# RMSNorm with SiLU: 48 KB blocks in four buffers, no look-ahead, and rstd moved from VectorE to the Silu

## Chip, cores, metric

One core of one Trainium2 chip. The time is the device time of one execution in microseconds (us). The profile's span (from the first to the last instruction) is 1.7 to 1.8 us shorter than the time of the same run. An execution of a one-core kernel is called slow when it is over 1.5% above the fastest of its kernel; all comparisons below use fast runs, except where it is said.

## The reference

```python
# x: (8, 1024, 2048) float32, gamma: (2048,), eps: 1e-5
rms = np.sqrt(np.mean(x ** 2, axis=-1, keepdims=True) + eps)
out = gamma * x / rms
return (out * (1 / (1 + np.exp(-out)))).astype(np.float32)
```

8192 rows of 2048 floats: 67.1 MB in, 67.1 MB out, and only a few operations per element.

## The kernel before

The rows are cut into 16 blocks of 512. Each of the 128 partitions holds four consecutive rows of a block, one run of 32 KB, and there are six such buffers. A load goes out on the queue of SyncE, a store on that of ScalarE. The order of work looks one block ahead: the square sums of block b+1 come before the multiplies of block b.

```python
J = 4
BUFS, LEAD = 6, 6
...
def sums(b, after_first=()):
    ...                                     # half of the rows on VectorE: sum of squares into ss
    for j in range(na):                     # the other half on ScalarE
        nc.scalar.activation(out=junk_a, in_=row(b, j), func=ACT.Square, accum_out=ss[:, j:j + 1])
        if j == 0:
            for s in after_first:
                store(s)                    # store of b-1 behind the first square of b+1
    nc.scalar.activation(out=rms, in_=ss, func=ACT.Sqrt, scale=1.0 / d, bias=eps_t)
...
def finish(b, halves=False):
    for j in range(J):
        nc.vector.scalar_tensor_tensor(out=row(b, j), in0=row(b, j), scalar=rstds[b][:, j:j + 1],
                                       in1=g, op0=ALU.mult, op1=ALU.mult)
        if j % 2:                           # Silu over two rows at once
            nc.scalar.activation(out=blocks[b][:, cols], in_=blocks[b][:, cols], func=ACT.Silu)
            ...                             # the last block is stored in two halves
def store(b):
    nc.scalar.dma_start(out=ob[b], in_=blocks[b])
    if b + LEAD < nblk:
        load(b + LEAD)
...
for b in range(1, last - 1):
    sums(b + 1, after_first=[b - 1])
    finish(b)
    invert(b + 1)                           # rstd = 1 / rms
```

Of the kernel before, what the change touches and what calls it, by code (L numbers as in the profile page):

```python
# [1 line left out]

# [4 lines left out]

ACT = mybir.ActivationFunctionType
ALU = mybir.AluOpType


@with_exitstack
def kernel(
    ctx: ExitStack,
    tc: tile.TileContext,
    x: bass.AP,
    gamma: bass.AP,
    eps: bass.AP,
    out: bass.AP,
):  # L20





    nc = tc.nc
    P = nc.NUM_PARTITIONS
    f32 = mybir.dt.float32
    x2 = x.flatten_outer_dims()
    o2 = out.flatten_outer_dims()  # L30
    n, d = x2.shape
    J = 4
    BUFS, LEAD = 6, 6
    nblk = n // (P * J)
    xb = x2.rearrange("(b p j) d -> b p (j d)", p=P, j=J)
    ob = o2.rearrange("(b p j) d -> b p (j d)", p=P, j=J)

    singles = ctx.enter_context(tc.tile_pool(name="singles", bufs=1))
    pool = ctx.enter_context(tc.tile_pool(name="pool", bufs=BUFS))
    small = ctx.enter_context(tc.tile_pool(name="small", bufs=2))  # L40
    psum = ctx.enter_context(tc.tile_pool(name="psum", bufs=1, space=bass.MemoryType.PSUM))

    g = singles.tile([P, d], f32)
    eps_t = singles.tile([P, 1], f32)
    ones = singles.tile([P, P], f32)
    junk_a = psum.tile([P, d], f32, name="junk_a")
    junk_v = psum.tile([P, d], f32, name="junk_v")
    blocks, rmss, rstds = {}, {}, {}

    def load(b):  # L50
        xt = pool.tile([P, J * d], f32, name="xt")
        nc.sync.dma_start(out=xt, in_=xb[b])  # L52
        blocks[b] = xt

    def row(b, j):
        return blocks[b][:, j * d:(j + 1) * d]

    def sums(b, after_first=()):


        ss = small.tile([P, J], f32, name="ss")
        na = J // 2
        for j in range(na, J):
            nc.vector.tensor_tensor_reduce(  # L64
                out=junk_v, in0=row(b, j), in1=row(b, j), scale=1.0, scalar=0.0,
                op0=ALU.mult, op1=ALU.add, accum_out=ss[:, j:j + 1])
        for j in range(na):
            nc.scalar.activation(out=junk_a, in_=row(b, j), func=ACT.Square,  # L68
                                 accum_out=ss[:, j:j + 1])
            if j == 0:  # L70
                for s in after_first:
                    store(s)
        rms = small.tile([P, J], f32, name="rms")
        nc.scalar.activation(out=rms, in_=ss, func=ACT.Sqrt, scale=1.0 / d, bias=eps_t)  # L74
        rmss[b] = rms

    def invert(b):
        rstd = small.tile([P, J], f32, name="rstd")
        nc.vector.reciprocal(out=rstd, in_=rmss.pop(b))  # L79
        rstds[b] = rstd  # L80

    def finish(b, halves=False):
        for j in range(J):
            nc.vector.scalar_tensor_tensor(out=row(b, j), in0=row(b, j), scalar=rstds[b][:, j:j + 1],  # L84
                                           in1=g, op0=ALU.mult, op1=ALU.mult)
            if j % 2:
                cols = slice((j - 1) * d, (j + 1) * d)
                nc.scalar.activation(out=blocks[b][:, cols], in_=blocks[b][:, cols], func=ACT.Silu)  # L88
                if halves:
                    nc.scalar.dma_start(out=ob[b][:, cols], in_=blocks[b][:, cols])  # L90

    def store(b):
        nc.scalar.dma_start(out=ob[b], in_=blocks[b])  # L93
        if b + LEAD < nblk:
            load(b + LEAD)

    with tc.manual_schedule():


        Q = 4  # L100
        w = d // Q
        grow = pool.tile([P, J * d], f32, name="xt")
        for b in range(BUFS - 1):
            load(b)
        nc.vector.memset(ones, 1.0)  # L105
        nc.vector.memset(eps_t, float(eps))  # L106
        nc.scalar.activation(out=junk_a[:, 0:1], in_=ones[:, 0:1], func=ACT.Square)  # L107
        nc.scalar.dma_start(out=grow[0:P:P // Q, 0:w],
                            in_=bass.AP(tensor=gamma.tensor, offset=gamma.offset, ap=[[w, Q], [1, w]]))
        for c in range(Q):  # L110
            k = c * (P // Q)
            nc.tensor.matmul(junk_v[:, c * w:(c + 1) * w], ones[k:k + 1, :], grow[k:k + 1, 0:w],  # L112
                             start=True, stop=True)
        nc.vector.tensor_copy(out=g, in_=junk_v)  # L114
        load(BUFS - 1)


        last = nblk - 1
        sums(0)
        invert(0)  # L120
        finish(0)
        sums(1)
        invert(1)
        for b in range(1, last - 1):
            sums(b + 1, after_first=[b - 1])
            finish(b)
            invert(b + 1)
        store(last - 2)
        finish(last - 1)
        store(last - 1)  # L130
        sums(last)
        invert(last)
        finish(last, halves=True)


# [1 line left out]
_INS = ['x', 'gamma', 'eps']  # L137
_OUTS = [((8, 1024, 2048), 'float32')]

_NUMBERS = {'eps': 9.999999747378752e-06}  # L140


# [26 lines left out]
```

## Time and profile before

| what | before |
|---|---|
| time, median | 317.8 us (317.19 to 318.23, 6 runs) |
| span of the profiled run | 316.3 us |
| share of the span that the DMA packets take | 49.7% + 49.2% |
| VectorE, ScalarE busy | 71%, 71% |
| median time from issue to landing of a load, of a store | 42.0 us, 35.2 us |

A transfer is called landed here at the last semaphore event that the trace has for it (in the kernel before 0.34 us after the end of the last packet of the first load). Read the two DMA shares first: they add to 98.9%, and nothing else is near that.

### The profile page before, as it was taken

How to read it: one execution, taken by the hardware profiler on the slowest of the kernel's cores; microseconds unless marked ns; L12 is line 12 of the kernel's file. 1: busy time of each engine (PE TensorE's matmuls, PEld its weight loads, DVE VectorE, ACT ScalarE, POOL GpSimd, SP SyncE). 2: the span in 40 equal slices, each digit the busy share in tenths (PEclk: the TensorE clock that was granted, in tenths of full speed). 3: DMA queues.
4: the chain of work that ended last, by engine and by line, in shares of the span. 5: the costliest groups of instructions: out<-in, count | busy, mean ns of one | idle time of the engine just before them, and what ended most of it. 6: DMA issues, size and time to landing. Idle time of an engine off the chain costs nothing.

```text
span 316.3 us, 444 instructions
## 1 busy us (share of the span) xinstructions
PE 2.1 (1%) x8; PEld 0.5 (0%) x8; DVE 223.5 (71%) x147; ACT 223.8 (71%) x144; POOL 0.2 (0%) x4
## 2 busy tenths in 40 slices
PE   0200000000000000000000000000000000000000
PEld 0000000000000000000000000000000000000000
DVE  0679499999493983939849397593966939993900
ACT  1357958999967777678676687676786776879540
POOL 0000000000000000000000000000000000000000
DMA  8999999999999999999999999999999999999996
GB/s 328 402 464 410 452 390 410 452 419 443 439 424 452 411 452 410 452 414 456 406 456 414 448 414 448 439 423 452 414 452 410 452 414 456 406 456 410 452 407 269
DMA packets 4763, 134.25 MB, mean 425 GB/s; under 512 B 532, under 2 KB 532, under 8 KB 536
## 3 DMA queue, kind: packets, MB, share of 16 engines
q1 hardware_dynamic: 2304, 67.11, 49.7%
q10 hardware_dynamic: 2456, 67.12, 49.2%
q14 instruction: 3, 0.02, 0.0%
HBM read 67.12 MB, written 67.11 MB: 424 GB/s over the span
## 4 chain that ended last, share of the span: by engine, by line
DMA 74%; DVE 14%; ACT 5%; issue 2%; DVEq 1%; ACTq 0%; SPq 0%
DMA xt<-in_x_dram 44%; DMA out_dram<-xt 30%; DVE xt L84 11%; ACT xt L88 3%; DVE junk_v L64 3%; ACT junk_a L68 1%; DVEq L164 1%; ACT L74 0%; ACT rms L74 0%; DVE rstd L79 0%; ACTq L93 0%; DVE ss L64 0%; SPq L52 0%; DVEq L64 0%; ACTq L74 0%
## 5 line engine op out<-in xcount | busy, mean ns | idle before, releaser
L84 DVE SCALAR_TENSOR_TENSOR xt<-xt,rstd,g 128x2048 f32<-128x2048 f32 x64 | 146.2, 2347 | 0.1
L88 ACT ACTIVATE xt<-xt 128x4096 f32<-128x4096 f32 x32 | 115.4, 3615 | 36.8 <-DVE xt L84 36.7
L64 DVE CUSTOM_DVE_ANT_0 junk_v<-xt 128x2048 f32<-128x2048 f32 x32 | 73.5, 2298 | 56.1 <-DMA xt<-in_x_dram 55.5
L68 ACT ACTIVATE junk_a<-xt 128x2048 f32<-128x2048 f32 x32 | 60.1, 1879 | 29.2 <-DMA xt<-in_x_dram 28.3
L74 ACT ACT_TABLE_LOAD x15 | 19.2, 1283 | 9.9 <-DVE ss L64 9.9
L88 ACT ACT_TABLE_LOAD x15 | 19.2, 1283 | 3.1 <-DVE xt L84 2.9
L79 DVE RECIPROCAL rstd<-rms 128x4 f32<-128x4 f32 x16 | 2.8, 172 | 11.3 <-ACT rms L74 11.3
L114 DVE COPY g<-junk_v 128x2048 f32<-128x2048 f32 x1 | 2.3, 2292 | 9.2 <-PE junk_v L112 9.2
L68 ACT ACTIVATION_READ_ACCUMULATOR junk_a<-xt 128x1 f32 x32 | 6.0, 186 | 0.0
L74 ACT ACTIVATE rms<-ss,eps_t 128x4 f32<-128x4 f32 x16 | 4.8, 297 | 1.2 <-DVE ss L64 1.1
L64 DVE DVE_READ_ACCUMULATOR2_ANT ss<- 128x1 f32 x32 | 4.5, 141 | 0.0
L112 PE MATMUL junk_v<-xt,ones 1*128 1x512 f32 x8 | 2.1, 1133 | 8.1 <-DMA xt<-in_gamma_dram 8.1
L107 ACT ACT_TABLE_LOAD x1 | 1.3, 1283 | 0.7 <-PEq L150 0.7
L105 DVE MEMSET ones<- 128x128 f32 x1 | 0.2, 165 | 0.8 <-PEq L150 0.8
L112 PEld LDWEIGHTS junk_v<-xt,ones 1*128 1x128 f32 x8 | 0.5, 306 | 8.1 <-issue 8.1
L107 ACT ACTIVATE junk_a<-ones 128x1 f32<-128x1 f32 x1 | 0.2, 174 | 0.0
L150 POOL MEMSET const-uint8-127<- 128x1 uint8 x1 | 0.1, 102 | 0.0
L150 POOL MEMSET const-bfloat16-1.0<- 128x1 bf16 x1 | 0.1, 101 | 0.0
L150 POOL MEMSET const-float32-0.0<- 128x1 f32 x1 | 0.1, 98 | 0.2 <-issue 0.2
L150 POOL MEMSET const-float32-1.0<- 128x1 f32 x1 | 0.1, 98 | 0.0
L106 DVE MEMSET eps_t<- 128x1 f32 x1 | 0.1, 59 | 0.0
## 6 DMA issues: line engine op xcount, KB each, us to landing
xt<-in_x_dram SPq DMA_DIRECT2D x16, 4096.0 KB, 42.0
out_dram<-xt ACTq DMA_DIRECT2D x15, 4096.0 KB, 35.2
out_dram<-xt ACTq DMA_DIRECT2D x2, 2048.0 KB, 10.4
xt<-in_gamma_dram ACTq DMA_DIRECT2D x1, 8.0 KB
```

The costliest lines, as they stand in the source:

```text
L64: nc.vector.tensor_tensor_reduce(out=junk_v, in0=row(b, j), in1=row(b, j), scale=1.0, scalar=0.0, op0=ALU.mult, op1=ALU.add, accum_out=ss[ ...
L68: nc.scalar.activation(out=junk_a, in_=row(b, j), func=ACT.Square, accum_out=ss[:, j:j + 1])
L74: nc.scalar.activation(out=rms, in_=ss, func=ACT.Sqrt, scale=1.0 / d, bias=eps_t)
L79: nc.vector.reciprocal(out=rstd, in_=rmss.pop(b))
L84: nc.vector.scalar_tensor_tensor(out=row(b, j), in0=row(b, j), scalar=rstds[b][:, j:j + 1], in1=g, op0=ALU.mult, op1=ALU.mult)
L88: nc.scalar.activation(out=blocks[b][:, cols], in_=blocks[b][:, cols], func=ACT.Silu)
L105: nc.vector.memset(ones, 1.0)
L107: nc.scalar.activation(out=junk_a[:, 0:1], in_=ones[:, 0:1], func=ACT.Square)
L112: nc.tensor.matmul(junk_v[:, c * w:(c + 1) * w], ones[k:k + 1, :], grow[k:k + 1, 0:w], start=True, stop=True)
L114: nc.vector.tensor_copy(out=g, in_=junk_v)
L150: nc = _bacc.Bacc("TRN2", target_bir_lowering=False, num_devices=1)
L164: with _tile.TileContext(nc) as tc:
```

## The change

Fewer and larger blocks: ten of 768 rows (six rows, 48 KB a partition) and one of 512, in four buffers. 4 x 48 KB is the same memory as 6 x 32 KB. The look-ahead goes: a block is worked on from its sums to its store before the next is begun. The wait that this opens on VectorE (for the Sqrt on ScalarE; 34.8 us in 11 waits in e12, 2.9 us in 3 in the changed kernel) is filled by a first multiply that doesn't need rstd: VectorE multiplies by gamma alone, and the Silu on ScalarE takes rstd as its scale, row by row.

```diff
-    J = 4
-    BUFS, LEAD = 6, 6
+    JMAX, BUFS = 6, 4
...
+    def work(b):
+        J = blks[b][1]
+        A = J // 2
+        for j in range(A):          # ScalarE: sums of squares of A rows
+            ...
+        for j in range(A, J):       # VectorE: of the others
+            ...
+        nc.scalar.activation(out=rms[:, 0:J], in_=ss[:, 0:J], func=ACT.Sqrt, scale=1.0 / d, bias=eps_t)
+        order = list(range(A, J)) + list(range(A))
+        for i, j in enumerate(order):
+            nc.vector.tensor_mul(out=row(b, j), in0=row(b, j), in1=g)
+            if i == 0:
+                nc.vector.reciprocal(out=rstd[:, 0:J], in_=rms[:, 0:J])
+            nc.scalar.activation(out=row(b, j), in_=row(b, j), func=ACT.Silu, scale=rstd[:, j:j + 1])
+            if b == nblk - 1 and i == J - A - 1:
+                store(b, A, J)
+        if b == nblk - 1:
+            store(b, 0, A)
+        else:
+            store(b, 0, J)
+        if b + BUFS < nblk:
+            load(b + BUFS)
...
-        for b in range(1, last - 1):
-            sums(b + 1, after_first=[b - 1])
-            finish(b)
-            invert(b + 1)
...
+        for b in range(nblk):
+            work(b)
```

More of the change, by code (lines that the diff above doesn't have):

```diff
@@ L31, with rows_of @@
     n, d = x2.shape
-    J = 4
-    BUFS, LEAD = 6, 6
-    nblk = n // (P * J)
-    xb = x2.rearrange("(b p j) d -> b p (j d)", p=P, j=J)
-    ob = o2.rearrange("(b p j) d -> b p (j d)", p=P, j=J)
+    JMAX, BUFS = 6, 4
+    blks = []
+    r = 0
+    while r < n:
+        j = JMAX if n - r >= JMAX * P else 4
+        blks.append((r, j))
+        r += j * P
+    nblk = len(blks)
+    def rows_of(t, b):
+        r0, J = blks[b]
+        return t[r0:r0 + P * J, :].rearrange("(p j) d -> p (j d)", p=P, j=J)
     singles = ctx.enter_context(tc.tile_pool(name="singles", bufs=1))
@@ L47 @@
     junk_v = psum.tile([P, d], f32, name="junk_v")
-    blocks, rmss, rstds = {}, {}, {}
+    blocks = {}
     def load(b):
-        xt = pool.tile([P, J * d], f32, name="xt")
-        nc.sync.dma_start(out=xt, in_=xb[b])
+        xt = pool.tile([P, JMAX * d], f32, name="xt")
+        nc.sync.dma_start(out=xt[:, 0:blks[b][1] * d], in_=rows_of(x2, b))
         blocks[b] = xt
@@ L56, in row, with store @@
         return blocks[b][:, j * d:(j + 1) * d]
-    def sums(b, after_first=()):
-        ss = small.tile([P, J], f32, name="ss")
-        na = J // 2
-        for j in range(na, J):
+    def store(b, j0, j1):
+        nc.scalar.dma_start(out=rows_of(o2, b)[:, j0 * d:j1 * d], in_=blocks[b][:, j0 * d:j1 * d])
+    def work(b):
+        J = blks[b][1]
+        A = J // 2
+        ss = small.tile([P, JMAX], f32, name="ss")
+        for j in range(A):
+            nc.scalar.activation(out=junk_a, in_=row(b, j), func=ACT.Square, accum_out=ss[:, j:j + 1])
+        for j in range(A, J):
             nc.vector.tensor_tensor_reduce(
@@ L66, in sums @@
                 op0=ALU.mult, op1=ALU.add, accum_out=ss[:, j:j + 1])
-        for j in range(na):
-            nc.scalar.activation(out=junk_a, in_=row(b, j), func=ACT.Square,
-                                 accum_out=ss[:, j:j + 1])
-            if j == 0:
-                for s in after_first:
-                    store(s)
-        rms = small.tile([P, J], f32, name="rms")
-        nc.scalar.activation(out=rms, in_=ss, func=ACT.Sqrt, scale=1.0 / d, bias=eps_t)
-        rmss[b] = rms
-    def invert(b):
-        rstd = small.tile([P, J], f32, name="rstd")
-        nc.vector.reciprocal(out=rstd, in_=rmss.pop(b))
-        rstds[b] = rstd
-    def finish(b, halves=False):
-        for j in range(J):
-            nc.vector.scalar_tensor_tensor(out=row(b, j), in0=row(b, j), scalar=rstds[b][:, j:j + 1],
-                                           in1=g, op0=ALU.mult, op1=ALU.mult)
-            if j % 2:
-                cols = slice((j - 1) * d, (j + 1) * d)
-                nc.scalar.activation(out=blocks[b][:, cols], in_=blocks[b][:, cols], func=ACT.Silu)
-                if halves:
-                    nc.scalar.dma_start(out=ob[b][:, cols], in_=blocks[b][:, cols])
-    def store(b):
-        nc.scalar.dma_start(out=ob[b], in_=blocks[b])
-        if b + LEAD < nblk:
-            load(b + LEAD)
+        rms = small.tile([P, JMAX], f32, name="rms")
+        rstd = small.tile([P, JMAX], f32, name="rstd")
+        nc.scalar.activation(out=rms[:, 0:J], in_=ss[:, 0:J], func=ACT.Sqrt, scale=1.0 / d, bias=eps_t)
[13 more added lines that the diff above has]
+            load(b + BUFS)
     with tc.manual_schedule():
@@ L101 @@
         w = d // Q
-        grow = pool.tile([P, J * d], f32, name="xt")
+        grow = pool.tile([P, JMAX * d], f32, name="xt")
         for b in range(BUFS - 1):
@@ L115 @@
         load(BUFS - 1)
-        last = nblk - 1
-        sums(0)
-        invert(0)
-        finish(0)
-        sums(1)
-        invert(1)
-        for b in range(1, last - 1):
-            sums(b + 1, after_first=[b - 1])
-            finish(b)
-            invert(b + 1)
-        store(last - 2)
-        finish(last - 1)
-        store(last - 1)
-        sums(last)
-        invert(last)
-        finish(last, halves=True)
+        for b in range(nblk):
+            work(b)
 _INS = ['x', 'gamma', 'eps']
```

## The prediction

The sum came to -0.1 us, from the completion packets alone (317.8 - 0.1 is 317.7; the forecast was written as 317.6). The 2.29 us of a plain multiply agrees with the fused one back to back (2.285 us). The rate is shared in halves because the two queues take 49.7% and 49.2% for equal bytes.

> **What bounds the kernel now.** I read the profile's page first, for which resource is full.
>
> ```profile
> DMA  8999999999999999999999999999999999999996
> DMA packets 4763, 134.25 MB, mean 425 GB/s; under 512 B 532, under 2 KB 532, under 8 KB 536
> q1 hardware_dynamic: 2304, 67.11, 49.7%
> q10 hardware_dynamic: 2456, 67.12, 49.2%
> ...
> DMA 74%; DVE 14%; ACT 5%; issue 2%; DVEq 1%; ACTq 0%; SPq 0%
> ```
>
> The strip has no hole: the 16 DMA engines are busy from the first slice to the last. The loads (q1) and the stores (q10) take 49.7% + 49.2% = 98.9% of the engines' span, which is 312.8 of 316.3 us. VectorE and ScalarE are busy 71% each. The 134.2 MB are the input read once and the output written once (2 x 67.1 MB); neither can shrink. So 312.8 us is a floor unless packets themselves become faster, and only 3.5 us of the span (1.1%) are anything else: the wait before the first packet, the uneven end, the last completion.
>
> Then the chain of waits in order of time, to see whether compute stands between transfers:
>
> ```profile
> 61.49 41.87 DMA xt<-in_x_dram
> 103.36 0.02 issue
> 103.39 0.03 ACT junk_a L68
> 103.41 0.04 issue
> 103.45 35.90 DMA out_dram<-xt
> 139.34 0.02 issue
> 139.36 0.03 SPq L52
> 139.39 0.03 issue
> 139.42 42.02 DMA xt<-in_x_dram
> ```
>
> A load ends, about 0.1 us later a store is issued, the store ends, and about 0.1 us later a load is issued into the buffer that it freed. A 4 MB block alone would need 4.19 MB / 432 GB/s (the rate of the packets, worked out under *DMAs*) = 9.7 us; it takes 36 to 42 because the transfers queue behind each other. These waits are a full queue seen from one transfer, not latency to be removed. Rates by stretch (us, then busy time by engine, clock, DMA share, GB/s):
>
> ```profile
> 10.00:36.00 26.00, 0.18 (x4) 0.00 (x0) 20.95 (x14) 17.37 (x12) 0.00 (x0) 1.00 1.00 430
> 60.00:300.00 240.00, 0.00 (x0) 0.00 (x0) 179.62 (x116) 182.00 (x114) 0.00 (x0) 1.00 1.00 434
> 290.00:316.30 26.30, 0.00 (x0) 0.00 (x0) 9.32 (x5) 10.19 (x6) 0.00 (x0) 1.00 0.88 380
> ```
>
> 10 to 36 us has loads only (the first store is issued at 36.7), 60 to 300 is mostly both: 430 and 434 GB/s. So mixing reads and writes costs nothing visible, and it does not matter when stores start, only that something is always queued.
>
> [...] q1 and q10 moving equal bytes in nearly equal time is consistent, and I use it to share the rate in halves. [...] its fused multiply takes 2347 ns alone and 9.14/4 = 2.285 us back to back. [...]
>
> **The change, part by part.** The costs on the compute engines come from these rows:
>
> ```profile
> L84 DVE SCALAR_TENSOR_TENSOR xt<-xt,rstd,g 128x2048 f32<-128x2048 f32 x64 | 146.2, 2347 | 0.1
> L88 ACT ACTIVATE xt<-xt 128x4096 f32<-128x4096 f32 x32 | 115.4, 3615 | 36.8 <-DVE xt L84 36.7
> L64 DVE CUSTOM_DVE_ANT_0 junk_v<-xt 128x2048 f32<-128x2048 f32 x32 | 73.5, 2298 | 56.1 <-DMA xt<-in_x_dram 55.5
> L68 ACT ACTIVATE junk_a<-xt 128x2048 f32<-128x2048 f32 x32 | 60.1, 1879 | 29.2 <-DMA xt<-in_x_dram 28.3
> L74 ACT ACT_TABLE_LOAD x15 | 19.2, 1283 | 9.9 <-DVE ss L64 9.9
> L88 ACT ACT_TABLE_LOAD x15 | 19.2, 1283 | 3.1 <-DVE xt L84 2.9
> ```
>
> *VectorE.* 64 fused multiplies of 2.29 us become 64 plain ones of 2.29 us: zero. Five fewer reciprocals of 0.17 us: -0.9.
>
> *ScalarE.* 16 blocks become 11 (ten of 768 rows, one of 512), so table loads go from 30 to about 22: 8 x 1.28 = -10.3 us. 32 Silus of 3.6 us become 64 of about 1.98 (1.88, the Square of the same width[...]): 126.7 - 115.4 = +11.3. Net about +1. Neither engine is the bound, so these are worth nothing directly.
>
> *Time per block without look-ahead.* Let VectorE start a six-row block at 0, as it ends the last multiply of the block before. Three square sums at 2.40 us start to start: 7.2. The first multiply needs no rstd: to 9.5. ScalarE ends the previous block's last Silu at 2.0, then three squares at 2.03: 8.1, table load and Sqrt 1.28 + 0.31: 9.7. The reciprocal waits 0.2 us: 9.9. Five multiplies of 2.29: 21.3. The last Silu: 23.3, then the store. So a block costs 21.3 us of cadence and 23.3 us from work to store. Its bytes are 2 x 6.29 MB; at 432 GB/s they cost 29.1 us. Dropping the look-ahead leaves about 8 us of slack a block: compute still follows the DMA.
>
> *Buffers.* 6 x 32 KB = 4 x 48 KB = 192 KB a partition: the same bytes in flight. Four buffers make a cycle of 4 x 29.1 = 116 us; compute holds one for 23, so each spends about 93 us loading, storing or queueing, where 2 x 14.6 us would do if it had the DMA alone. On average 93/29.1 = 3.2 transfers' worth is pending. The DMA can run dry only if all four wait for compute at once.
>
> *Start.* The first load took 12.37 us for 4.19 MB; 2.10 MB more adds 4.9, so it lands at 18.0 instead of 13.1. Adding the work: sums to 25.2, table load and Sqrt to 26.8, reciprocal and the last multiply at about 39, Silu and store at 41 (36.7 now). Meanwhile four loads (25.2 MB, 58 us) are queued. The later store only shifts writes; queued reads fill the gap: zero.
>
> *End.* At 41 us the reads have moved about 38.3 us x 432 GB/s = 16.5 MB. Sharing in halves from there, reads end with 16.5 MB still to write, or 38 us before a last packet near 314: 276. Block 9 landed about 19 us before that (4.19 MB at half rate), at 257, and its work ends near 280. The last block's sums, square root and two rows take to about 290, all of it to 295. Its last 2.1 MB (4.9 us) must join the queue by about 309. The slack is 14 us; the kernel before issues its last at 304.8, hence nearly at the limit but not beyond it.
>
> *DMAs.* 16 loads and 17 stores become 11 and 12: 10 fewer, each with 16 four-byte completion packets. In the trace's packet records these average 9 ns: 160 x 9 / 16 = -0.1 us. 32 KB packets of 1213 ns in the steady state (27.0 GB/s an engine, x16 = 432) become 48 KB packets, expected at 1.82 us.
>
> The sum is -0.1 us on the path. I add nothing for the other parts.
>
> **The rivals.** First, *compute becomes the bound* because a block's work is now serial between engines. It would need over 29.1 us a block against my 21.3; at 32 us I would get 11 x 32 + 20 = 370. VectorE's longest waits today (55.5 us on loads) say there is idle time to spend; against it I see only that the chain now crosses ScalarE twice a block. 2%. Second, *coarser buffers starve the loads*: a load now waits for a whole 6 MB store. The pool of pending bytes argues against it, and an empty load queue leaves the engines to the stores. If each of the last seven reloads left the DMA idle 1 us: 325. 1 to 2%. Third, *48 KB runs move differently*. [...] Worse: 1% less would be 321. Nothing in this trace tests the size; this is the main width of my range. Fourth, *the early finish of compute trims the end*: the 380 GB/s of the last 26.3 us against 434 are 3.3 us, but most of it is the emptying and the last completion, which stay. At most -1 us.
>
> **Range and chances.** Time before 317.8, minus 0.1: 317.6. The measured spread is 0.6 us; the packet size and the end give 1 us each down, and 2 up. Range 316.3 to 319.4. Faster than 311.4 [...] Chance 1%. Slower than 324.2 needs a rival: 3%.
>
> **What would show it.** Right: the DMA strip stays full, the two queues' shares sum to about 99%, the middle gives 432 to 434 GB/s; the first store is issued near 41 us, the last near 295, with stores still draining; table loads number about 22; VectorE waits for loads, some 8 us a block. Wrong: a digit below 9 in the middle of the strip, waits of ScalarE and VectorE for each other above those for loads (compute bound), an x load issued with both queues empty, or a packet rate away from 432 GB/s with the strip full.

## The result, and the profile after

The changed kernel takes 317.55 us (median of 6 runs, 317.4 to 319.21), the kernel before 317.81 us in 6 runs. The ratio of the fast runs is 1.0004 with a 95% interval of 0.9981 to 1.0027: the same time. (Ratios here are the mean time of one kernel's fast runs over that of the other's from the same rounds, so not quite the ratio of the medians.) One run took 319.21 us; the kernel before has none above 318.23. One run is too little to make anything of.

From the page of the changed kernel, the same rows as in the prediction. The first is the DMA strip: each digit is the busy share, in tenths, of the 16 DMA engines in one of 40 equal slices of the span. In an engine's row stand, behind the count, its busy time (us), the mean time of one instruction (ns), the idle time before it, and what ended that:

```profile
DMA  8999999999999999999999999999999999999996
q1 hardware_dynamic: 1584, 67.11, 49.7%
q10 hardware_dynamic: 1736, 67.12, 49.2%
...
L83 DVE TENSOR_TENSOR xt<-xt,g 128x2048 f32<-128x2048 f32 x64 | 142.4, 2279 | 0.0
L86 ACT ACTIVATE xt<-xt,rstd 128x2048 f32<-128x2048 f32 x64 | 125.3, 1996 | 4.5 <-DVE xt L83 3.2
L75 DVE CUSTOM_DVE_ANT_0 junk_v<-xt 128x2048 f32<-128x2048 f32 x32 | 73.6, 2299 | 60.2 <-DMA xt<-in_x_dram 59.5
L73 ACT ACTIVATE junk_a<-xt 128x2048 f32<-128x2048 f32 x32 | 60.2, 1882 | 58.0 <-DMA xt<-in_x_dram 56.0
```

The strip is the same digit for digit and the two shares are the same, with 30% fewer packets. Both engines now wait for loads and hardly for each other: the Silu waited 36.7 us for VectorE before, 3.2 now. The stretches (us, busy time by engine, clock, DMA share, GB/s):

```profile
10.00:36.00 26.00, 0.68 (x4) 0.00 (x0) 19.70 (x13) 16.14 (x13) 0.00 (x0) 1.00 1.00 433
60.00:300.00 240.00, 0.00 (x0) 0.00 (x0) 176.15 (x114) 181.74 (x133) 0.00 (x0) 1.00 1.00 434
290.00:315.60 25.60, 0.00 (x0) 0.00 (x0) 2.67 (x2) 4.63 (x3) 0.00 (x0) 1.00 0.88 381
```

434 GB/s in the middle, as before, and 381 for 380 at the end, although hardly any arithmetic is left there. The chain of waits in the middle:

```profile
134.03 0.33 SPq L59
134.35 28.62 another core or an unknown queue
162.97 0.02 SPq L59
163.00 0.03 issue
163.03 0.33 SPq L59
```

SyncE issues a load at 134.03 and the next at 163.03. The profile can't name what lies between, hence the label; there is only one core here. The period, 29.0 us, is what the DMA needs for one block's 12.6 MB, so I read it as the wait for a store to land; the list of SyncE's waits says the same (236.6 us in 7 waits for stores). No piece of this stretch of the chain is arithmetic.

### The profile page after: what moved, and what is told of

The parts are those of the page before. It is cut to its first block, busy times and chain, and to the rows that moved or that the text cites. A ratio compares the mean times of both kernels' runs of the same rounds, so it can differ in the third digit from the quotient of the medians.

```text
span 315.6 us, 421 instructions
## 1 busy us (share of the span) xinstructions
PE 2.1 (1%) x8; PEld 0.5 (0%) x8; DVE 219.0 (69%) x142; ACT 222.4 (70%) x163; POOL 0.2 (0%) x4
## 3 DMA queue, kind: packets, MB, share of 16 engines
q1 hardware_dynamic: 1584, 67.11, 49.7%
q10 hardware_dynamic: 1736, 67.12, 49.2%
## 4 chain that ended last, share of the span: by engine, by line
another core or an unknown queue 45%; DMA 28%; DVE 11%; ACT 6%; issue 1%; SPq 1%; ACTq 0%; DVEq 0%
DMA xt<-in_x_dram 15%; DMA out_dram<-xt 14%; DVE xt L83 8%; ACT xt L86 4%; DVE junk_v L75 4%; ACT junk_a L73 2%; SPq L59 1%; ACT L80 0%; ACT L86 0%; ACTq L66 0%; ACT rms L80 0%; DVE ss L75 0%; DVE rstd L85 0%; DVEq L75 0%
## 5 line engine op out<-in xcount | busy, mean ns | idle before, releaser
L83 DVE TENSOR_TENSOR xt<-xt,g 128x2048 f32<-128x2048 f32 x64 | 142.4, 2279 | 0.0
L86 ACT ACTIVATE xt<-xt,rstd 128x2048 f32<-128x2048 f32 x64 | 125.3, 1996 | 4.5 <-DVE xt L83 3.2
L75 DVE CUSTOM_DVE_ANT_0 junk_v<-xt 128x2048 f32<-128x2048 f32 x32 | 73.6, 2299 | 60.2 <-DMA xt<-in_x_dram 59.5
L85 DVE RECIPROCAL rstd<-rms 128x6 f32<-128x6 f32 (+1 forms) x11 | 2.0, 184 | 2.9 <-ACT rms L80 2.9
L80 ACT ACTIVATE rms<-ss,eps_t 128x6 f32<-128x6 f32 (+1 forms) x11 | 3.3, 299 | 0.1
## 6 DMA issues: line engine op xcount, KB each, us to landing
out_dram<-xt ACTq DMA_DIRECT2D x10, 6144.0 KB, 46.5
xt<-in_x_dram SPq DMA_DIRECT2D x1, 4096.0 KB, 29.1
```

The lines of the kernel that those rows point to most:

```text
L75: nc.vector.tensor_tensor_reduce(out=junk_v, in0=row(b, j), in1=row(b, j), scale=1.0, scalar=0.0, op0=ALU.mult, op1=ALU.add, accum_out=ss[ ...
L80: nc.scalar.activation(out=rms[:, 0:J], in_=ss[:, 0:J], func=ACT.Sqrt, scale=1.0 / d, bias=eps_t)
L83: nc.vector.tensor_mul(out=row(b, j), in0=row(b, j), in1=g)
L85: nc.vector.reciprocal(out=rstd[:, 0:J], in_=rms[:, 0:J])
L86: nc.scalar.activation(out=row(b, j), in_=row(b, j), func=ACT.Silu, scale=rstd[:, j:j + 1])
```

## The experiments

The diffs below are cut to what matters (`...`). The theory after the result: the bytes set the time, and the arithmetic has about 8 us to spare in each block. The first rival: the halves of the change cost and gain, and cancel. The second: the compute is near its limit, so that the equality is luck.

### e1: the new order and arithmetic in the old sizes

```diff
-    JMAX, BUFS = 6, 4
+    JMAX, BUFS = 4, 6
```

> The new work order with the old sizes: 16 blocks of four rows (32 KB a partition) in six buffers. Theory (the DMA engines set the time, both halves of the change are hidden): 317.9, that is the kernel before within 0.5 us, DMA strip full. Rival (two effects that cancel: dropping the look-ahead costs time and the larger blocks win it back): slower than the kernel before by clearly more than 1 us, with holes in the DMA strip or VectorE and ScalarE waiting for each other more than for loads.

317.49 us, ratio to the kernel before 0.9996 (0.9983 to 1.0010), DMA strip full (134.2 MB in a span of 316.0 us, 425 GB/s on average). In the old sizes the old order with the old arithmetic is worth no more than the new with the new.

### e2: the old order and arithmetic in the new sizes

```diff
-    J = 4
-    BUFS, LEAD = 6, 6
+    JMAX = 6
+    BUFS, LEAD = 4, 4
...                              # blocks as in the changed kernel
```

> The old work order (look-ahead, fused multiply, Silu on two rows) with the new sizes: eleven blocks, 48 KB a partition, four buffers. Theory: 317.5, equal to the changed kernel within 0.5 us. Rival (two effects that cancel): clearly faster than the changed kernel, by more than 1 us. A store of block b-1 is issued only after the first square of block b+1, so fewer bytes are pending; if this bites, holes in the DMA strip and some us slower.

324.56 us, ratio 1.0207 (1.0185 to 1.0228). The theory's number is missed by 7 us, and the rival's sign too: large blocks in four buffers lose under the old order and arithmetic. The clause on pending bytes in the expectation came true. From the chain of this kernel:

```profile
106.09 30.51 DMA xt<-in_x_dram
136.60 0.02 issue
136.63 28.91 DMA out_dram<-xt
...
```

A 6.29 MB transfer at half of 432 GB/s takes 29.1 us, and here loads and stores take about that (medians 30.5 and 29.1 us): each has nothing ahead of it in its own queue. In the changed kernel a store takes 46.5 us (median), because it stands behind another. Without a queue, every landing leaves one of the two queues empty until its next transfer is going. Five stretches of e2, two long ones and three short (a stretch counts the bytes of the packets that start in it, so a short one can show a little too much or too little):

```profile
74.00:120.00 46.00, 0.00 (x0) 0.00 (x0) 30.18 (x21) 30.14 (x21) 0.00 (x0) 1.00 0.98 399
120.00:280.00 160.00, 0.00 (x0) 0.00 (x0) 118.05 (x73) 110.64 (x64) 0.00 (x0) 1.00 1.00 426
...
82.00:88.00 6.00, 0.00 (x0) 0.00 (x0) 6.00 (x4) 5.94 (x6) 0.00 (x0) 1.00 0.78 270
88.00:104.00 16.00, 0.00 (x0) 0.00 (x0) 6.04 (x4) 8.67 (x3) 0.00 (x0) 1.00 1.02 439
136.00:140.00 4.00, 0.00 (x0) 0.00 (x0) 3.24 (x3) 3.35 (x3) 0.00 (x0) 1.00 1.02 442
```

The changed kernel moves 436 and 434 GB/s in these stretches: (436 - 399) x 46 / 434 = 3.9 us and (434 - 426) x 160 / 434 = 2.9 us, together 6.8 of the 7.5 us between the two spans.

The packet records of two places show where it goes. Here an empty queue alone cost nothing: from 136 to 140 us only stores move, at 442 GB/s. From 82 to 88 us the loss falls where a transfer starts on a queue that was empty: the load issued at 78.39 has its first packet at 83.8 us (5.4 us after its issue; in e8, where at 56.75 nothing else moves, it is 1.0), packets around it are recorded with up to 3.7 us for 1.8, and the rate is 270 GB/s. Over the run the packets of e2 take 5.8 us more of each engine's time than those of the changed kernel (318.1 for 312.3); only 1.6 us more are idle. So the strip and the two shares stay high although the rate falls. Why a start costs this much, no run shows.

Why is nothing queued? VectorE multiplies block b only behind the sums of block b+1, and the store of b goes out behind the first square of b+2. So a block that landed at 195.2 was stored at 255.0: 59.8 us, two block periods, of a cycle of 4 x 29.1 = 116.4 us. The 57 us left hold one load and one store at half rate (58.2 us) and no more. In the changed kernel a block that landed at 225.9 was stored at 248.3, after 22.4 us.

### e3: no arithmetic

The whole body of the block's work is taken out; each block is loaded and stored. Its output is wrong, which doesn't matter for the time.

> The changed kernel with all block arithmetic removed: load, store, nothing between; the output is x and wrong on purpose. Theory: the bytes alone set the time, so 316.5 to 317.5, not more than 1 us below the changed kernel. Rival (compute still shows in the time, at the start, the end or between): 310 to 314.

318.0 us, ratio 1.0013 (1.0000 to 1.0026). A copy of the same bytes by the same transfers isn't faster. In its profile one DMA engine ends at 315.4 us and the others by 313.8 (packets joined into one chain for each engine, as in e12 below), which accounts for the 1.0 us that its span is longer than that of the changed kernel. The arithmetic of the changed kernel is hidden. A copy with the transfers of the kernel before was not run, but that kernel takes the same time. So 317 to 318 us is what this way of moving the bytes takes, and no run with any arithmetic went below it by more than the spread.

### e4: pieces of 8 KB

Row r of a block goes to partition r mod 128; the load and the store are changed to match (not shown).

```diff
-        return t[r0:r0 + P * J, :].rearrange("(p j) d -> p (j d)", p=P, j=J)
+        return t[r0:r0 + P * J, :].rearrange("(j p) d -> p j d", p=P, j=J)
...
```

> The changed kernel with row r of a block on partition r mod 128, so that each transfer moves 8 KB pieces and not 48 KB runs; bytes and arithmetic are the same. In the packet records 16 KB took 611 ns and 32 KB 1213 ns: 602 ns per 16 KB and 9 ns fixed. 16384 data packets for 2944 now: 13440 x 9 ns / 16 engines = 7.6 us more. Theory with this fixed cost: 325. Rival (a packet costs only its bytes): 317.5. [...]

320.5 us, ratio 1.0092 (1.0079 to 1.0106): between the two. The spans differ by 318.8 - 315.6 = 3.2 us (e4 less the changed kernel). If all of it comes from the 13,440 more packets, each costs 3.2 x 16 / 13,440 = 3.8 ns, not 9. (The edit also changes the order of the addresses in memory; that part was not taken apart.) The records give the 8 KB packets 310 ns on average, 9 more than half of the 602 ns that 16 KB add; but their sum, 317.8 us an engine, is longer than the 315.8 us in which they ran, so neighbours overlap in the records. The fixed part that counts is then the smaller one, 3.8 ns at most. From 32 to 48 KB it is worth 1280 packets x 3.8 / 16 = 0.3 us: lost in the spread of the runs.

### e5 and e6: more work for VectorE

```diff
+        for _ in range(3):          # e6: 6
+            nc.vector.tensor_mul(out=junk_v, in0=g, in1=g)
```

> The changed kernel with three more multiplies of 128x2048 per block on VectorE, into a scratch tile. A block's cadence in the changed trace is 21.4 us where it has no load to wait for; 21.4 + 3 x 2.29 = 28.3, still below the 29.0 us that the DMA takes for a block. Theory: 317.6, unchanged within 0.5 us, VectorE waits for loads nearly gone. Rival (compute is already partly on the path): up to 11 x 6.9 = 75 us slower, and several us at least.

317.27 us, ratio 0.9993 (0.9976 to 1.0009). VectorE is busy 93% of the span and the time doesn't move. Its waits for loads fall from 59.5 us to 5.5, all of it before the first block. A block takes VectorE 27.3 us here and not the 28.3 of the expectation (its square sums start at 18.56, 45.84, 73.12 us and so on): the extra multiplies also fill a wait of 1.0 us for the Sqrt. The last store is issued at 307.3 us, close to the 309 that the prediction had for too late, and still nothing is lost.

> Six more multiplies per block: cadence 21.4 + 6 x 2.29 = 35.1 us, above the 29.0 us of the DMA. Theory: VectorE becomes the bound: first block at 18.5, ten cadences 351, the last block to its last Silu 16, its last store 7, and 1.9 between span and time: 394; holes in the DMA strip. If it stayed at 318, the slack would be far larger than I think; well above 400, the extra work would cost more than its durations.

391.3 us, ratio 1.2325 (1.2307 to 1.2343), 3 us below the expected 394. The nearness is partly luck: a block takes 34.3 us and not 35.1, which over ten blocks makes 8 us, so the other terms were 5 us too small. (The 7 us of the last store was an estimate; one of that size took 7.0 us from issue to landing in e9, 6.3 in e10.) From its page:

```profile
DVE  0399999999999999999999999999999999999998
ACT  1189808933980794298079429907942990693460
POOL 0000000000000000000000000000000000000000
DMA  8999999999999989989998997999899059019363
```

The full row has changed places: VectorE has no hole and the DMA strip has many. Between them the two runs put the limit between 27.3 and 34.3 us a block, where the theory has 29.0. Against the 21.4 us of the changed kernel the slack is at least 5.9 us a block and less than 12.9. The second rival is out.

### e7 and e8: three and two buffers

> The changed kernel with three buffers of 48 KB (144 KB a partition). Cycle 3 x 29.1 = 87 us, compute holds a buffer for 23, so 64/29.1 = 2.2 transfers' worth pending on average. Theory: the middle stays full; the last load lands later, so the last store is close to too late: 317.5 to 321. Rival (four buffers are just enough, starving begins at once): 330 or more.

The fast runs took 322.98 and 323.3 us, two others 329.63 and 331.48; ratio of the fast runs 1.0178 (1.0157 to 1.0198). Both expectations miss. The stretches of a fast run show why 317.5 to 321 was too low:

```profile
60.00:80.00 20.00, 0.00 (x0) 0.00 (x0) 18.96 (x14) 18.99 (x16) 0.00 (x0) 1.00 0.95 378
80.00:120.00 40.00, 0.00 (x0) 0.00 (x0) 22.01 (x14) 24.34 (x17) 0.00 (x0) 1.00 1.00 433
120.00:280.00 160.00, 0.00 (x0) 0.00 (x0) 109.38 (x72) 110.10 (x82) 0.00 (x0) 1.00 1.00 432
280.00:300.00 20.00, 0.00 (x0) 0.00 (x0) 18.00 (x12) 18.73 (x14) 0.00 (x0) 1.00 0.86 369
```

The middle is full, as expected; the start loses (433 - 378) x 20 / 433 = 2.5 us and the end (433 - 369) x 20 / 433 = 3.0 us. Why some runs lose 7 us more stays open; they have no profile.

> The changed kernel with two buffers of 48 KB. One buffer alone needs 23 us of work and two transfers of 14.6 us[...], 56 us a cycle of two blocks against 58 us of DMA work for them; the two buffers also collide. Theory: now the DMA runs dry: 335 to 375 with holes in the strip. Rival (buffers don't matter as long as there are two): 318 to 325.

364.88 us, ratio 1.1484 (1.1456 to 1.1513), inside the expected band. Its 56 us a cycle held a time for two transfers to be seen to land; without it 23 + 2 x 14.6 makes 52. With two buffers the 134.2 MB take 362.9 us of span, a mean of 370 GB/s for 425 in the changed kernel, and VectorE waits 119.6 us for loads (10 waits) and not 59.5. In this kernel, where a block is loaded, worked on and stored in one buffer, two buffers are 15% too slow.

### e9: the look-ahead with the store ahead of the squares

From e2 I made a theory: what counts is the time for which a buffer is held, in block periods. If so, e2 should recover when the store no longer waits for the next landing.

The diff is against e2:

```diff
         na = J // 2
+        for s in after_first:
+            store(s)
...
-            if j == 0:
-                for s in after_first:
-                    store(s)
```

> As e2_big_lookahead, but ScalarE issues the store of block b-1 before its first square of block b+1, not after it. In e2 the block was finished at 219.7 us and its store issued at 227.9, the moment the next load landed. New theory: the look-ahead order holds a buffer for two block periods plus about 2 us (2 x 29.1 + 2 = 60 of 4 x 29.1 = 116), which leaves 56 us where a load and a store at half rate need 58; 8 us earlier leaves 64, so the DMA stays full: 317.5 to 318.5. Rival (the look-ahead itself, two blocks of compute in a row, costs the time): still 322 to 325.

324.68 us, ratio 1.0224 (1.0200 to 1.0248): nothing recovered. The theory's number fails and the rival's comes true. Some time is gained in a buffer's holding (in the profiled run a block landed at 228.9 and was stored at 285.4, 56.5 us), but less than 8 us, since the multiplies still wait for the sums of the next block. Where the fast runs lose I can't say: the profiled run is a slow one (328.3 us), and its holes aren't used as evidence.

### e10 and e11: the kernel before with four and five of its buffers

```diff
-    BUFS, LEAD = 6, 6
+    BUFS, LEAD = 4, 4           # e11: 5, 5
```

> The kernel before with four buffers of 32 KB and nothing else changed. Block period 19.4 us. Theory (what counts is the number of buffers against two held periods): cycle 77.7, held 2 x 19.4 + 2 = 41, left 37 where a load and a store at half rate need 38.8, so as in e2, with 16 blocks for 11: 7 x 16/11 = 10 us, about 328. Rival (48 KB blocks are what hurts the look-ahead order): 317.6 to 319.

> The kernel before with five buffers of 32 KB. Cycle 97, held 41, left 56 against 38.8: one block period spare. Theory: 317.6, within 0.5 us. Rival (every buffer fewer costs): 320 to 323.

Four buffers: 329.11 us, ratio 1.0357 (1.0334 to 1.0380), for an expected 328. Five: 317.6 us, ratio 1.0007 (0.9995 to 1.0019), for an expected 317.6. The issue rows of the page, with the median time to landing at the end of the row, tell them apart; first with four buffers, then with five:

```profile
xt<-in_x_dram SPq DMA_DIRECT2D x16, 4096.0 KB, 20.3
out_dram<-xt ACTq DMA_DIRECT2D x15, 4096.0 KB, 18.5
```

```profile
xt<-in_x_dram SPq DMA_DIRECT2D x16, 4096.0 KB, 25.0
out_dram<-xt ACTq DMA_DIRECT2D x15, 4096.0 KB, 31.3
```

At half rate 4.19 MB take 19.4 us. With four buffers both take about that: no queue, as in e2. With five there is one, and the DMA is full (134.2 MB in a span of 316.4 us are 424 GB/s on average, for 425 in the kernel before). So the 48 KB blocks aren't what hurts the look-ahead: four buffers are too few for it at either size, and 160 KB in five are enough where 192 KB in four (e2) aren't. Five of 48 KB were not run.

### e12: the changed kernel with the old arithmetic

```diff
-            nc.vector.tensor_mul(out=row(b, j), in0=row(b, j), in1=g)
-            if i == 0:
-                nc.vector.reciprocal(out=rstd[:, 0:J], in_=rms[:, 0:J])
-            nc.scalar.activation(out=row(b, j), in_=row(b, j), func=ACT.Silu, scale=rstd[:, j:j + 1])
+            nc.vector.scalar_tensor_tensor(out=row(b, j), in0=row(b, j), scalar=rstd[:, j:j + 1],
+                                           in1=g, op0=ALU.mult, op1=ALU.mult)   # reciprocal before the loop
+            if j % 2:                                                           # rows in order 0, 1, 2, ...
+                nc.scalar.activation(out=blocks[b][:, cols], in_=blocks[b][:, cols], func=ACT.Silu)
...                                                                             # last store in halves, as the rows come
```

> The changed kernel with the old arithmetic: reciprocal first, then fused multiply by rstd and gamma on VectorE, Silu over two rows without scale. Without the look-ahead the first multiply now waits for the Sqrt: a block's cadence grows from 21.4 by one multiply, about 2.3, to 23.7, still below 29.0. Theory: 317.6, within 0.5 us, with VectorE waiting longer for ScalarE and less for loads. Rival (the new operations are worth time): 319 or more.

325.14 us, ratio 1.0226 (1.0202 to 1.0249), and all six runs lie between 323.06 and 325.66. The theory missed. It isn't the cadence: with the first two blocks' data there, VectorE starts them at 40.97 and 66.66, 25.7 us apart, more than the 23.7 expected, but e5 with its 27.3 costs nothing. Nor is the queue empty: a store takes 39.7 us to land (median). The loss is at the end:

```profile
300.00:312.00 12.00, 0.00 (x0) 0.00 (x0) 4.01 (x2) 6.75 (x2) 0.00 (x0) 1.00 0.97 414
...
314.00:316.00 2.00, 0.00 (x0) 0.00 (x0) 0.00 (x0) 0.00 (x0) 0.00 (x0) 1.00 0.17 74
316.00:318.00 2.00, 0.00 (x0) 0.00 (x0) 0.00 (x0) 0.00 (x0) 0.00 (x0) 1.00 0.15 66
318.00:321.00 3.00, 0.00 (x0) 0.00 (x0) 0.00 (x0) 0.00 (x0) 0.00 (x0) 1.00 0.13 55
```

From 314 to 321 us the DMA share is 0.17, then 0.15 and 0.13, and 2/16 is 0.125: fourteen of the sixteen DMA engines are done and two are still writing. In the changed kernel the last packets of all sixteen end within about 1.5 us of each other. There each engine moves the same 8.4 MB (8.39 to 8.41 in its sixteen chains, joined as below); taking the same here, these two fell back some 7 us on the way. In the records single packets, most of them of loads, are stretched by 0.06 to 1.3 us, scattered from 49 to 278 us after the first packet (some 76 in that time, against 4 after 48 us in the changed kernel). The records carry no number of the engine, but packets follow each other within some ns, so they can be joined into one chain for each engine. The two chains that end at 321.5 and 322.2 us have 8.2 and 9.2 us of such stretching after 47 us, the others 0.5 to 2.7. So the stretched packets are what made the two engines late, in this one profile. What in the old arithmetic brings this about (the fused multiply, the wide Silu, the order of the rows or the later store) was not tried and stays open.

## Why the prediction was right

The time was forecast as 317.6 us and is 317.55. Its steps against the trace:

| step | predicted | measured |
|---|---|---|
| DMA shares, sum | about 99% | 49.7% + 49.2% |
| rate in the middle | 432 to 434 GB/s | 434 |
| a 48 KB packet | 1.82 us | 1.815 us (median) |
| first load lands, first store issued | 18.0, 41 us | 18.4, 41.0 us |
| cadence of a block without a wait for a load | 21.3 us | 21.4 us (38.80 to 60.16) |
| plain multiply of one row | 2.29 us | 2.279 us (mean) |
| Silu of one row with scale | 1.98 us | 1.996 us |
| table loads | about 22 | 22, and the warm-up's |
| last load lands; last two stores issued | 276; 290, 295 us | 279; 290.8, 295.1 us |
| VectorE's waits for loads | some 8 us a block | 59.5 us in 8 waits |

- *The bound.* Bytes set the time: shown by e3 (no arithmetic, no gain) and by e5 (more arithmetic, no loss).
- *The work per block.* That there is slack, of 5.9 to 12.9 us a block where the prediction had about 8, is shown by e5 and e6, which lie on either side of the limit. (The rival's 11 x 32 + 20 makes 372, not 370.)
- *Start and end.* Both went as worked out. The last store is issued about 10 us earlier in its kernel than before (295.1 for 304.8), and the end is no shorter: the last stretch moves 381 GB/s for 380. The rival that the end is trimmed did not come about.
- *Packets.* The -0.1 us of the sum came from completion packets; the fixed part of the 1280 data packets saved would take off about 0.3 us more, by e4. It was not in the sum. Neither can be seen in the runs.
- *Buffers.* Here the reasoning was weaker than the number. "The same bytes in flight" is no argument by itself: e2 has the same bytes and loses 7 us. What carried the step was its other half, a buffer held for 23 us of 116. That the look-ahead with four buffers holds one for 60 was not seen, nor was it needed. That the DMA can lose only when all four buffers wait for compute is wrong: e2 loses at the start of a transfer (270 GB/s from 82 to 88 us), with a load or a store under way in other buffers.
- *The arithmetic.* It was counted as zero because its engine time is hidden. e12 shows that with the new blocks it isn't neutral, through two late DMA engines and not through the engine time that was counted. The prediction's zero held for the whole change; for this part taken away alone it fails, and why is open. The prediction gave no reason why the new blocks and order would need the new arithmetic, so here the right number was luck.

So both rivals of the experiments are out as they stood, but the parts of the change do depend on each other: four large buffers lost time with the old order and arithmetic (e2) and with the new order and the old arithmetic (e12), and keep it with both new; the old order with the new arithmetic was not run. No run is faster than the kernel before by more than the spread, the copy of e3 included.

## What to carry to other kernels

When the strip of the DMA is full, its packets' time sums to 99% of the span and the rate in the middle (434 GB/s here) is held throughout, count how much work the others can take on before they become the limit, and don't pay for rearranging them. The strip alone isn't enough: the shares of e2 add to 98.5%, and it loses 2%. A copy with the arithmetic removed shows in one run what the transfers alone take (318.0 us in e3). Count buffers in block periods and not in bytes, and take off the periods for which the order of work holds a buffer. One load and one store at half rate fill two periods (2 x 29.1 us of 29.1 in e2's sizes, by the bytes). Here 1.9 (e2, e10) and 2.2 (e7) periods left cost 2 to 4%, and 2.9 (e11) and 3.2 (the changed kernel) nothing (estimates from the block periods and the times for which a buffer is held); but e12 loses with its stores queued, so this is not enough alone. The time to landing helps: equal to the transfer's time at half rate meant, in e2 and e10, that nothing stood behind it, and these two kernels lost 2.1% and 3.6%; in e2 part of the loss was seen at the start of a transfer.
